# Low parts taken one half-block later at a stage's seam, and a fixed order for the last two tiles before the feed-forward part

## The chip, the cores and the metric

The kernel runs on one core of a Trainium2 chip. The time is device microseconds of that core for one launch, and a smaller time is better. Every time in this text is in microseconds unless it says ns.

The engines that matter here are TensorE (PE in the profile; PEld is its weight load), VectorE (DVE), ScalarE (ACT) and GpSimd (POOL). SyncE (SP) issues the transfers. Each engine takes its instructions in the order in which the program holds them for it, and an instruction waits on semaphores of the other engines and of transfers.

## The reference

One layer of a hybrid block works on 1024 tokens of width 1024 (16 meta tokens lead), all in float32. After a norm, one wide product gives the inputs of a pooling mixer and of a chunked, gated linear attention; both are merged under sigmoid gates and multiplied with `w_out`. A squared-ReLU feed-forward part of width 4096 and a last norm follow.

```python
h = h + hybrid_mixer(rmsnorm(h, norm_mix), ...)
#   y_a = pooling branch                      y_b = (attention output o) @ w_gla_out
#   m = sigmoid(ga) * y_a + sigmoid(gb) * y_b
#   returns m @ w_out
h = h + square(relu(rmsnorm(h, norm_ffn) @ w_ff1)) @ w_ff2
out = rmsnorm(h, norm_final)[:, N_META:]
```

## The kernel before

**Numbers.** A float32 value is kept as two parts that TensorE takes at full rate: a high part, which is a copy by ScalarE into a rounded type, and a low part, which is value minus high part, by VectorE (in some places by GpSimd). A product then is three matmuls for each 128 rows: high × high, low × high, high × low (`mm3`, L255 to L257 for the row numbers of its three matmuls). In the names, `th`/`tl` are high and low part of activations, `w1h`/`w1l` of weights in a ring of two slots (`Ring`, L83 and L87), `wo` holds both parts of half of `w_out`.

**The seam.** It lies between the attention and the product with `w_out`. `yb_block(n, h)` computes two blocks of 128 columns of `m` for the token half `h`; I call one of these a half-block (one value of `e`). It is 12 matmuls on `yg`, then on VectorE a multiplication with the gate (L1115), an addition of the pooling branch (L1116), the high part by ScalarE (L1119) and the low part, for `h = 1` by VectorE (L1121), for `h = 0` by GpSimd in four pieces (L1123). Gate and pooling branch are loaded from DRAM into buffers of three slots (`yb_load`, L1061 and L1062). In the second half, steps of `load_wo` stand between the blocks: each turns a quarter of the first half of `w_out` into its two parts (L1422, L1423). The third and fourth block of the second half need a new weight from the ring. After eight half-blocks, `out_tile` multiplies tile after tile of 128 tokens with `w_out`, first for columns 0 to 511 (`ch = 0`), then for the others.

**The opening of the feed-forward part.** In `out_tile` for `ch = 1` a tile is finished: its result is added to x (L1455), normed by `layer_norm` (L243 to L247), and two tiles later transposed by TensorE (`turn_tile`, L1472). The product with `w_ff1` is computed by a scheme with seven products of quarters instead of eight (P1 to P7, class `Quarters`), each 12 matmuls for half the rows of a block of 128 columns (4 times 128 rows, three matmuls each). Its operands are sums and differences of the four quarters of activations, so `turn_tile` for tiles 4 to 7 also computes differences: `t1` (L1482), which with its two parts (L1483, L1484) P5 reads, and after it four more arrays (L1477, L1486 to L1492) that only P6, P7 and P4 read. The weights' sums are made by `sums` and their two parts by `split` (L273, L274). For each weight pair the order is P1 P1 P2 P2 P5 P5 P6 P7 P4 P3 at the start. The last two tiles (6 and 7) are transposed between the first products, in `ff_layers`.

**What sets the order.** TensorE's order is that of the code. On the other engines a scheduler orders by its own estimates, except inside `in_order(...)` ... `any_order(...)`, where ScalarE, VectorE or SP also keep the order of the code. From the end of the attention to `wo1_open` ScalarE and VectorE are in such a stretch; `x_again`, `fetch_wo` and the loads around them are in one for SP. In the opening of the feed-forward part there is none.

Of the kernel before, what the change touches and what calls it, by code (L numbers as in the profile page):

```python
# [114 lines left out]
def kernel(  # L115
# [84 lines left out]
    def f32(ap):  # L200
        return ap.bitcast(F32)
# [4 lines left out]
    def bcast(v):  # L206
        return v[None, :].broadcast_to([P, D])
# [80 lines left out]
    class Quarters:  # L288
# [46 lines left out]
        def forms(self):  # L335

            for p, i, s in ahead(self.sums(), self.lead):
                yield p, i, split(s)
                if p == "P3" and i + 2 < self.n:
                    self.load(i + 2, 0)  # L340
                    self.load(i + 2, 1)
# [742 lines left out]

    kept = {}
    halves_of_half = [slice(k * HALF // 2, (k + 1) * HALF // 2) for k in range(2)]

    def yb_block(n, h):
        j = YB[h][n]

        def fn(*wbs):
# [6 lines left out]
            for e in range(2):  # L1098
                d, w = 2 * j + e, slice(e * P, (e + 1) * P)
                for m in range(2 + h):  # L1100
                    yb_load(2 * n + e + m, h)
                gl, ml = staged[2 * n + e, h]
                b = bank("mm")
                for k in range(4):
                    mm3(
                        b, 1, lambda i: (hi[:, k, w], lo[:, k, w]),
                        lambda i: (yg[:, 0, k], yg[:, 1, k]), first=k == 0, last=k == 3,
                    )
                    yield 3 * 512 / 2400
                if e and not wbs:  # L1110
                    W1.done, W1.kept = W1.done + 1, W1.kept - 1
                    W1.top_up()
                elif e:
                    yield "keep" if j in kept else "free"
                dve.tensor_tensor(gl, b, gl, ALU.mult)  # L1115
                dve.tensor_tensor(gl, gl, ml, ALU.add)  # L1116
                th = MH[h][:, d]
                tl = ML[h][:, d]
                act.activation(th, gl, ACT.Copy)  # L1119
                if h:  # L1120
                    dve.tensor_tensor(tl, gl, f32(th), ALU.subtract)  # L1121
                for c in halves_of_half[: 2 - 2 * h]:
                    pool.tensor_tensor(tl[:, c], gl[:, c], f32(th[:, c]), ALU.subtract)  # L1123
# [274 lines left out]

    def load_gB():
        nc.sync.dma_start(gB, bcast(norm_ffn))  # L1400

# [15 lines left out]
    def load_wo(ch, kk):  # L1417
        def fn():
# [3 lines left out]
            act.activation(wo[:, 0], r, ACT.Copy)  # L1422
            dve.tensor_tensor(wo[:, 1], r, f32(wo[:, 0]), ALU.subtract)  # L1423

# [36 lines left out]

    def turn_tile(t, tags=("ms",)):

# [16 lines left out]
        b12, t1 = (quad(acc[:, t, c]) for c in halves())  # L1480
        act.activation(b12, b[0], ACT.Copy)
        dve.tensor_tensor(t1, b[0], lo, ALU.subtract)  # L1482
        act.activation(MH[1][:, 0:4, cols], t1, ACT.Copy)  # L1483
        dve.tensor_tensor(ML[1][:, 0:4, cols], t1, f32(MH[1][:, 0:4, cols]), ALU.subtract)  # L1484
        split_from_psum(MH[1][:, 4:8, cols], ML[1][:, 4:8, cols], b[1])
        dve.tensor_tensor(lo, b[1], t1, ALU.subtract)  # L1486
        dve.tensor_tensor(b12, b[1], b12, ALU.subtract)
        dve.tensor_tensor(hi, hi, lo, ALU.subtract)
        for n, a in enumerate((lo, b12)):
            fh, fl = (S["wo"][0][:, k, 4 * n : 4 * n + 4, cols] for k in range(2))  # L1490
            act.activation(fh, a, ACT.Copy)
            dve.tensor_tensor(fl, a, f32(fh), ALU.subtract)  # L1492

# [27 lines left out]
    for t in ORDER[:6]:  # L1521
        step(one, out_tile(t, 1))
    step(one, lambda: ff_weights())
    for t in ORDER[6:]:
        step(one, out_tile(t, 1))
# [193 lines left out]
    def ff_layers():  # L1719
# [3 lines left out]
        run = ff_quarters.run()  # L1723
        for n in range(4):
            if n in (1, 3):
                turn_tile(ORDER[6 + n // 2])
            next(run)
# [53 lines left out]
```

## Time and profile before

| | us |
|---|---|
| median of 3 runs | 1224.9 |
| the runs | 1224.36 to 1225.51 |
| the profiled execution | 1225.56 |
| its span | 1222.7 |
| TensorE busy | 1202.0 |
| VectorE busy | 853.9 |
| ScalarE busy | 618.9 |
| GpSimd busy | 62.7 |

The profiled execution is one execution of the program, recorded by the hardware; its span runs from the first to the last instruction, and the execution's own time is 2.86 longer. Busy time of TensorE is the time in which a matmul is under way, and matmuls overlap, so that a matmul of 512 columns is recorded with 0.39 although the next one starts much sooner. Whether TensorE stands still is therefore read from the distance between starts. In a row of the timeline stand the start, the duration, the engine, the line, the operation, output and inputs with their shape, and in brackets how long the engine sat idle before it and who ended that.

In this trace the first half-block of the second token half reaches TensorE at about 484, the product with `w_out` starts at 506.67, the feed-forward part at 601.81.

### The profile page before, as it was taken

What the parts mean: (1) busy time and instruction counts of PE and PEld (TensorE: products, weight loads), DVE (VectorE), ACT (ScalarE), POOL (GpSimd) and SP (SyncE); (2) the same over time, 40 slices, a digit from 0 to 9 for tenths busy, and PEclk for the clock granted to TensorE, in tenths of its full rate; (3) what the DMA queues carried; (4) which work ended last, traced back from release to release, by engine and by line L of the source; (5) the groups of instructions that cost most, each with busy time, mean ns of one, the idle gap of its engine ahead of it and who ended that gap; (6) DMA issues with size and microseconds to landing.
All of it is one profiled execution on the core that took longest, in us unless ns stands there. A gap on an engine that the chain in (4) does not pass through costs nothing.

```text
span 1222.7 us, 18359 instructions
## 1 busy us (share of the span) xinstructions
PE 1202.0 (98%) x6818; PEld 1000.4 (82%) x6818; DVE 853.9 (70%) x1399; ACT 618.9 (51%) x1099; POOL 62.7 (5%) x100
## 2 busy tenths in 40 slices
PE   7999999999999999999999999999999999999997
PEld 7878888978888877788878888888888888888886
DVE  7986675754566677735887676676775887887686
ACT  7667567322546753323655455454554444444544
POOL 2000000001201225000000000000000000000000
PEclk9999999999999999999999999999999999999999
DMA  8043426156101246651244454444569973333532
GB/s 254 2 113 116 125 86 190 53 161 201 36 20 62 70 159 213 234 179 63 104 144 155 134 168 147 155 155 139 175 223 322 341 249 102 96 95 95 171 96 86
DMA packets 141672, 173.84 MB, mean 142 GB/s; under 512 B 9944, under 2 KB 81392, under 8 KB 141584
## 3 DMA queue, kind: packets, MB, share of 16 engines
q1 hardware_dynamic: 141552, 172.62, 43.6%
q8 instruction: 53, 0.87, 0.3%
q14 instruction: 35, 0.29, 0.1%
q0 software_dynamic: 32, 0.07, 0.0%
HBM read 119.17 MB, written 53.48 MB: 141 GB/s over the span
## 4 chain that ended last, share of the span: by engine, by line
PE 87%; DVE 7%; ACT 2%; issue 2%; DMA 1%; POOL 0%; SPq 0%; DVEq 0%; ACTq 0%; POOLq 0%
PE b_mm L255 10%; PE b_mm L256 10%; PE b_mm L257 10%; PE b_ms L256 9%; PE b_ms L255 9%; PE b_ms L257 9%; PE b_x L256 8%; PE b_x L255 8%; PE b_x L257 8%; PE b_sc L1207 1%; PE b_mx L255 1%; PE b_mx L256 1%; PE b_mx L257 1%; PE b_m L1309 1%; DVE ut L776 1%
## 5 line engine op out<-in xcount | busy, mean ns | idle before, releaser
L255 PE MATMUL b_mm<-th,w1h 128*128 128x512 f32 (+1 forms) x312 | 117.6, 377 | 1.6 <-DVE c L811 1.0
L256 PE MATMUL b_mm<-tl,w1h 128*128 128x512 f32 (+1 forms) x312 | 116.0, 372 | 0.6 <-DVE tl L1484 0.6
L257 PE MATMUL b_mm<-th,w1l 128*128 128x512 f32 (+1 forms) x312 | 115.9, 371 | 0.0
L255 PE MATMUL b_x<-th,w1h 128*128 128x512 f32 (+1 forms) x240 | 90.8, 378 | 0.0
L256 PE MATMUL b_x<-tl,w1h 128*128 128x512 f32 (+1 forms) x240 | 90.6, 378 | 0.0
L257 PE MATMUL b_x<-th,w1l 128*128 128x512 f32 (+1 forms) x240 | 90.3, 376 | 0.0
L273 ACT ACTIVATE w1h<-raw 128x512 fp32r<-128x512 f32 x96 | 59.5, 621 | 32.6 <-PE b_x L256 14.2
L274 DVE TENSOR_TENSOR w1l<-raw,w1h 128x512 fp32r<-128x512 f32 x96 | 65.6, 684 | 9.9 <-ACT w1h L273 9.9
L255 PEld LDWEIGHTS b_mm<-th,w1h 128*128 128x128 f32 x312 | 58.6, 188 | 13.2 <-issue 1.4
L273 ACT ACTIVATE w1h<-fs 128x512 fp32r<-128x512 f32 x72 | 45.4, 630 | 46.3 <-PE b_ms L256 31.8
L256 PEld LDWEIGHTS b_mm<-tl,w1h 128*128 128x128 f32 x312 | 58.6, 188 | 10.7 <-DVE tl L1484 0.9
L257 PEld LDWEIGHTS b_mm<-th,w1l 128*128 128x128 f32 x312 | 58.6, 188 | 10.3
L273 ACT ACTIVATE w1h<-bt 128x512 fp32r<-128x512 f32 x44 | 27.8, 632 | 67.1 <-issue 62.7
L274 DVE TENSOR_TENSOR w1l<-fs,w1h 128x512 fp32r<-128x512 f32 x72 | 49.3, 686 | 14.7 <-ACT w1h L273 14.6
L1638 DVE TENSOR_TENSOR bt<-w,w 128x512 f32<-128x512 f32 x80 | 54.6, 683 | 1.6 <-DMA w<-in_w_ff_dram 1.6
L257 PEld LDWEIGHTS b_x<-th,w1l 128*128 128x128 f32 x240 | 45.1, 188 | 8.5
L255 PEld LDWEIGHTS b_x<-th,w1h 128*128 128x128 f32 x240 | 45.1, 188 | 8.4
L256 PEld LDWEIGHTS b_x<-tl,w1h 128*128 128x128 f32 x240 | 45.1, 188 | 8.3
L273 ACT ACTIVATE fxh<-bt 128x512 fp32r<-128x512 f32 x36 | 22.8, 632 | 55.7 <-issue 50.1
L255 PE MATMUL b_ms<-wo,w1h 128*128 128x512 f32 x128 | 49.8, 389 | 0.0
L256 PE MATMUL b_ms<-wo,w1h 128*128 128x512 f32 x128 | 49.8, 389 | 0.0
L257 PE MATMUL b_ms<-wo,w1l 128*128 128x512 f32 x128 | 49.8, 389 | 0.0
(451 smaller groups left out, 3349.2 us busy)
## 6 DMA issues: line engine op xcount, KB each, us to landing
hf_dram<-h SPq DMA_DIRECT2D x112, 256.0 KB, 2.1
raw<-hf_dram SPq DMA_DIRECT2D x112, 256.0 KB, 2.6
w<-in_w_ff_dram SPq DMA_DIRECT2D x64, 256.0 KB, 4.7
raw<-in_w_in_dram SPq DMA_DIRECT2D x24, 512.0 KB, 4.8
raw<-in_w_ff_dram SPq DMA_DIRECT2D x16, 512.0 KB, 4.1
rawx<-in_w_ff_dram SPq DMA_DIRECT2D x16, 512.0 KB, 4.0
xs<-in_x_dram SPq DMA_DIRECT2D x8, 512.0 KB, 5.6
rawx<-in_w_in_dram SPq DMA_DIRECT2D x8, 512.0 KB, 4.4
```

Of the source, the lines that this page charges most:

```text
L255: pe.matmul(ps, ah, bh, start=first and i == 0, stop=False, skip_group_check=more)
L256: pe.matmul(ps, ah, bl, start=False, stop=False, skip_group_check=more)
L257: pe.matmul(ps, al, bh, start=False, stop=last and i == n - 1, skip_group_check=more)
L273: act.activation(hi, a, ACT.Copy)
L274: dve.tensor_tensor(lo, a, f32(hi), ALU.subtract)
L776: dve.tensor_tensor(to_, a_, b_, ALU.subtract)
L1207: pe.matmul(b[to, e, j], kk[r, s], qq[r, s], start=True, stop=True, tile_position=(e * CH, u * CH))
L1309: pe.matmul(o[part(u), e, j], scc[part(u), e, j], v[part(u), j, e], start=j == 0, stop=False, tile_position=(u * CH, u * CH), skip_group_c ...
L1638: dve.tensor_tensor(bt, w, S["w2"][q[3:]][:, i], ALU.add if q[2] == "+" else ALU.subtract)
```

## The change

The change has three parts.

First, in the seam, low parts are put into a list `pending` instead of being issued: that of a half-block of the second half (L1121 before), and those of `w_out` (L1423 before). `late()` issues what is in the list. It is called behind the multiplication of the next half-block; for the second half of `w_out` it is called at once, and the last one is issued before `gB` is loaded. The third load ahead for a half-block moves behind this point as well, since its buffer is what the late low part reads, and the ring's refill now stands between multiplication and addition.

VectorE, in the second half: the last row of the third weight block of the ring (`w1l`) and the half-blocks after it; `t` is a half-block's buffer, `o` the pooling branch. Before:

```order
L87 TENSOR_TENSOR w1l<-raw_115,w1h 128x1024
L1115 TENSOR_TENSOR t_4555<-b_mm,t_4555 128x512
L1116 TENSOR_TENSOR t_4555<-t_4555,o_4559 128x512
L1121 TENSOR_TENSOR tl_143<-t_4555,th_139 128x512
L1423 TENSOR_TENSOR wo_4843<-acc,wo_4843 128x1024
```

Now:

```order
L87 TENSOR_TENSOR w1l<-raw_115,w1h 128x1024
L1134 TENSOR_TENSOR t_4555<-t_4555,o_4559 128x512
L1124 TENSOR_TENSOR t_4555<-b_mm,t_4555 128x512
L1139 TENSOR_TENSOR tl_143<-t_4555,th_139 128x512
L1442 TENSOR_TENSOR wo_4843<-acc,wo_4843 128x1024
L1134 TENSOR_TENSOR t_4555<-t_4555,o_4559 128x512
```

Between a half-block's addition (now L1134) and its low part (now L1139) the multiplication of the next one (now L1124) stands, and that one's own addition comes only behind the weight's low part.

The first quarter of `w_out` is loaded early, and its low part stood on VectorE among the last half-blocks of the first token half, ahead of the sum of squares of the last attention part (L1331). Before:

```order
L1314 COPY small<-b_m_4670 128x2
L1115 TENSOR_TENSOR t_2709<-b_mm,t_2709 128x512
L1423 TENSOR_TENSOR wo_4843<-raw_4563,wo_4843 128x1024
L1116 TENSOR_TENSOR t_2709<-t_2709,o 128x512
L1331 TENSOR_REDUCE small<-mix 128x8
```

Now VectorE has it behind the first multiplication of the second half:

```order
L1133 TENSOR_TENSOR t_2709<-b_mx,t_2709 128x512
L1134 TENSOR_TENSOR t_2709<-t_2709,o 128x512
L1124 TENSOR_TENSOR t_4555<-b_mm,t_4555 128x512
L1442 TENSOR_TENSOR wo_4843<-raw_4563,wo_4843 128x1024
L1134 TENSOR_TENSOR t_4555<-t_4555,o_4559 128x512
```

It moved past the whole end of the attention, to where GpSimd still makes low parts of the first half.

Second, ScalarE and VectorE keep the order of the code from the last two tiles of `out_tile` to the third product of the feed-forward part. Third, in that stretch `turn_tile` leaves the differences that P6, P7 and P4 read to a function that is called later, `forms` can make a weight's sum ahead on demand (`pull`), and the last tile's transposes stand one product earlier on TensorE: behind the second P1 and no longer behind the first P2.

VectorE at the opening, from the last tile's norm (`u`, tile 7) on; `fs` is a sum of weights, the row of L1482 (now L1502) makes `t1`. Before (tile 6's `t1` stands just ahead of the piece):

```order
L247 SCALAR_TENSOR_TENSOR u_5026<-acc,small,gB 128x1024
L1484 TENSOR_TENSOR tl_143<-acc,th_139 128x4x128
L211 TENSOR_TENSOR tl_143<-b_ms,th_139 128x4x128
L1486 TENSOR_TENSOR acc<-b_ms,acc 128x512
L1487 TENSOR_TENSOR acc<-b_ms,acc 128x512
L1488 TENSOR_TENSOR acc<-acc 128x512
L1492 TENSOR_TENSOR wo_4843<-acc,wo_4843 128x4x128 x2
L274 TENSOR_TENSOR w1l<-fs,w1h 128x512
L1482 TENSOR_TENSOR acc<-b_ms,acc 128x512
L211 TENSOR_TENSOR tl_143<-b_ms,th_139 128x4x128
L1486 TENSOR_TENSOR acc<-b_ms,acc 128x512
L1484 TENSOR_TENSOR tl_143<-acc,th_139 128x4x128
```

Now:

```order
L247 SCALAR_TENSOR_TENSOR u_5026<-acc,small,gB 128x1024
L324 TENSOR_TENSOR fs<-raw_119 128x512
L1502 TENSOR_TENSOR acc<-b_ms,acc 128x512
L1504 TENSOR_TENSOR tl_143<-acc,th_139 128x4x128
L211 TENSOR_TENSOR tl_143<-b_ms,th_139 128x4x128
L274 TENSOR_TENSOR w1l<-fs,w1h 128x512
L1502 TENSOR_TENSOR acc<-b_ms,acc 128x512
L326 TENSOR_TENSOR fs<-fs,raw_115 128x512
L1504 TENSOR_TENSOR tl_143<-acc,th_139 128x4x128
L211 TENSOR_TENSOR tl_143<-b_ms,th_139 128x4x128
L324 TENSOR_TENSOR fs<-rawx_5695 128x512
L1509 TENSOR_TENSOR acc<-b_ms,acc 128x512
```

The low part of the last tile's `t1` (now L1504) stood behind tile 6's differences (L1486 to L1492) and is now ahead of them; both tiles' differences follow from the last row on, and the low parts for P4 (`t4l`, L1550 before), which stood ahead of P6's weight, now stand behind it.

The diff:

```diff
         def forms(self):
-            for p, i, s in ahead(self.sums(), self.lead):
+            due, made = [], self.sums()
+            self.pull = lambda: due.append(next(made))
+            while True:
+                while len(due) <= self.lead and (x := next(made, None)):
+                    due.append(x)
+                if not due:
+                    return
+                p, i, s = due.pop(0)
                 yield p, i, split(s)
...
-    kept = {}
+    kept, pending = {}, []
+
+    def late():
+        while pending:
+            pending.pop(0)()
...
-                for m in range(2 + h):
+                for m in range(2):
                     yb_load(2 * n + e + m, h)
...
+                if h:
+                    dve.tensor_tensor(gl, b, gl, ALU.mult)
+                    late()
+                    yb_load(2 * n + e + 2, h)
                 if e and not wbs:
                     W1.done, W1.kept = W1.done + 1, W1.kept - 1
                     W1.top_up()
                 elif e:
                     yield "keep" if j in kept else "free"
-                dve.tensor_tensor(gl, b, gl, ALU.mult)
+                if not h:
+                    dve.tensor_tensor(gl, b, gl, ALU.mult)
                 dve.tensor_tensor(gl, gl, ml, ALU.add)
...
                 if h:
-                    dve.tensor_tensor(tl, gl, f32(th), ALU.subtract)
+                    pending.append(lambda tl=tl, gl=gl, th=th: dve.tensor_tensor(tl, gl, f32(th), ALU.subtract))
...
     def load_gB():
+        late()
         nc.sync.dma_start(gB, bcast(norm_ffn))
...
             act.activation(wo[:, 0], r, ACT.Copy)
-            dve.tensor_tensor(wo[:, 1], r, f32(wo[:, 0]), ALU.subtract)
+            pending.append(lambda: dve.tensor_tensor(wo[:, 1], r, f32(wo[:, 0]), ALU.subtract))
+            if ch:
+                late()
...
-    def turn_tile(t, tags=("ms",)):
+    def turn_tile(t, tags=("ms",), later=None):
...
-        act.activation(b12, b[0], ACT.Copy)
         dve.tensor_tensor(t1, b[0], lo, ALU.subtract)
         act.activation(MH[1][:, 0:4, cols], t1, ACT.Copy)
         dve.tensor_tensor(ML[1][:, 0:4, cols], t1, f32(MH[1][:, 0:4, cols]), ALU.subtract)
         split_from_psum(MH[1][:, 4:8, cols], ML[1][:, 4:8, cols], b[1])
-        dve.tensor_tensor(lo, b[1], t1, ALU.subtract)
...
+        act.activation(b12, b[0], ACT.Copy)
+
+        def differences():
+            dve.tensor_tensor(lo, b[1], t1, ALU.subtract)
+            dve.tensor_tensor(b12, b[1], b12, ALU.subtract)
+            dve.tensor_tensor(hi, hi, lo, ALU.subtract)
+            for n, a in enumerate((lo, b12)):
+                fh, fl = (S["wo"][0][:, k, 4 * n : 4 * n + 4, cols] for k in range(2))
+                act.activation(fh, a, ACT.Copy)
+                dve.tensor_tensor(fl, a, f32(fh), ALU.subtract)
+
+        if later is None:
+            differences()
+        else:
+            later.append(differences)
...
     step(one, lambda: ff_weights())
+    step(one, lambda: in_order("order", mybir.EngineType.Activation, mybir.EngineType.DVE))
     for t in ORDER[6:]:
         step(one, out_tile(t, 1))
...
-        for n in range(4):
-            if n in (1, 3):
-                turn_tile(ORDER[6 + n // 2])
+        later = []
+        for n in range(5):
+            if n == 1:
+                ff_quarters.pull()
+                turn_tile(ORDER[6], later=later)
+            elif n == 2:
+                turn_tile(ORDER[7], later=later)
+                ff_quarters.pull()
+                later[0]()
+            elif n == 3:
+                later[1]()
+                any_order("order")
             next(run)
```

More of the change, by code (lines that the diff above doesn't have):

```diff
@@ L1485, in turn_tile @@
         split_from_psum(MH[1][:, 4:8, cols], ML[1][:, 4:8, cols], b[1])
-        dve.tensor_tensor(lo, b[1], t1, ALU.subtract)
[L1487 to L1492, printed above, removed]
+        act.activation(b12, b[0], ACT.Copy)
[11 more added lines that the diff above has]
+            later.append(differences)
     for n, j in enumerate(YB[1]):
```

## The prediction

> **What bounds the kernel now.** I read the head of the page and its chain first, then the list of waits of TensorE, then the timelines of TensorE, VectorE, ScalarE and GpSimd around the two places that the change touches. Times inside the trace are microseconds from the start of the span.
>
> ```profile
> span 1222.7 us, 18359 instructions
> PE 87%; DVE 7%; ACT 2%; issue 2%; DMA 1%; POOL 0%; SPq 0%; DVEq 0%; ACTq 0%; POOLq 0%
> ```
>
> TensorE carries the chain. Only time in which it stands still can be won, and the list of its waits shows single waits of under a microsecond, two of them at the lines of the change:
>
> ```profile
> PE b_mm L256 <- DVE wo L1423: 0.8, 1, 0.8
> PE b_mm L256 <- DVE tl L1484: 0.6, 1, 0.6
> ```
>
> A wait costs more than its own length, since the first matmul after it is spaced wider. So I measure from start to start. The seam, on TensorE:
>
> ```profile
> 484.34 0.39 PE L255 MATMUL b_mm<-yg,w1h 128*128 128x512 f32 x1
> 485.04 0.50 PE L256 MATMUL b_mm<-yg,w1h 128*128 128x512 f32 x1 [0.31 <-DVE yg L1341]
> 485.38 0.39 PE L257 MATMUL b_mm<-yg,w1l 128*128 128x512 f32 x1
> ...
> 499.46 0.39 PE L256 MATMUL b_x<-yg,w1h 128*128 128x512 f32 x1
> 499.68 0.39 PE L257 MATMUL b_x<-yg,w1l 128*128 128x512 f32 x1
> 500.27 0.50 PE L255 MATMUL b_x<-yg,w1h 128*128 128x512 f32 x1 [0.20 <-ACT w1h L83]
> ...
> 501.53 0.50 PE L257 MATMUL b_x<-yg,w1l 128*128 128x512 f32 x1 [0.53 <-DVE w1l L87]
> 501.86 0.40 PE L255 MATMUL b_x<-yg,w1h 128*128 128x512 f32 x1
> ...
> 510.52 0.39 PE L257 MATMUL b_mm<-wo,tl 128*128 128x512 f32 x1
> 511.38 0.50 PE L255 MATMUL b_mm<-wo,th 128*128 128x512 f32 x1 [0.47 <-ACT wo L1422]
> 512.64 0.50 PE L256 MATMUL b_mm<-wo,th 128*128 128x512 f32 x1 [0.76 <-DVE wo L1423]
> 512.98 0.40 PE L257 MATMUL b_mm<-wo,tl 128*128 128x512 f32 x1
> ```
>
> Undisturbed matmuls follow each other at 0.227 (499.46 to 499.68, and the like all over). Lost are therefore: at yg 485.38 − 484.34 − 2 × 0.227 = 0.59; at the third weight block 501.86 − 499.68 − 4 × 0.227 = 1.27; at the last quarter of w_out 512.98 − 510.52 − 3 × 0.227 = 1.78. That is **3.64 in the seam**. The feed-forward opening:
>
> ```profile
> 597.31 0.39 PE L257 MATMUL b_mm<-wo,tl 128*128 128x512 f32 x1
> 598.16 1.06 PE L1472 MATMUL b_ms<-ident,u 128*128 128x128 f32 x8 [0.46 <-DVE small L220]
> ...
> 614.28 0.39 PE L257 MATMUL b_x<-th,w1l 128*128 128x512 f32 x1
> 615.28 0.49 PE L255 MATMUL b_mm<-th,w1h 128*128 128x512 f32 x1 [0.61 <-ACT th L1483]
> 616.41 0.50 PE L256 MATMUL b_mm<-tl,w1h 128*128 128x512 f32 x1 [0.64 <-DVE tl L1484]
> 616.75 0.40 PE L257 MATMUL b_mm<-th,w1l 128*128 128x512 f32 x1
> ```
>
> Before the transposes 598.16 − 597.31 − 0.227 = 0.62 is lost; at the fifth product (P5) 616.75 − 614.28 − 3 × 0.227 = 1.79. All five together are 6.05, 0.5% of the span: no more than that can be won here. The profiled execution took 1225.56, 0.66 above the median of 1224.9; I take the difference from the trace and put it on the median.
>
> **The change, part by part.**
>
> *Low parts taken one half-block later.* One half-block of before on VectorE and ScalarE, and a half-block without a weight behind it:
>
> ```profile
> 501.39 0.68 DVE L1115 TENSOR_TENSOR t<-b_mm,t 128x512 f32<-128x512 f32 x1
> 502.11 0.69 DVE L1116 TENSOR_TENSOR t<-t,o 128x512 f32<-128x512 f32 x1
> 502.83 0.63 ACT L1119 ACTIVATE th<-t 128x512 fp32r<-128x512 f32 x1 [2.62 <-DVE t L1116]
> 503.37 1.04 ACT L1422 ACTIVATE wo<-acc 128x1024 fp32r<-128x1024 f32 x1
> 504.45 1.23 DVE L1423 TENSOR_TENSOR wo<-acc,wo 128x1024 fp32r<-128x1024 f32 x1 [0.26 <-ACT wo L1422]
> 505.59 0.68 DVE L1115 TENSOR_TENSOR t<-b_mm,t 128x512 f32<-128x512 f32 x1
> ...
> 507.70 0.69 DVE L1121 TENSOR_TENSOR tl<-t,th 128x512 fp32r<-128x512 f32 x1 [0.70 <-ACT th L1119]
> 508.31 0.68 DVE L1115 TENSOR_TENSOR t<-b_x,t 128x512 f32<-128x512 f32 x1
> ```
>
> The period of VectorE is 505.59 − 501.39 = 4.20 with a weight and 508.31 − 505.59 = 2.72 without; TensorE's is 12 × 0.227 = 2.72. So every weight puts VectorE 1.48 further behind, which is why the last quarter of w_out is late. In the period VectorE stands idle 0.70 for the high part of the block and 0.26 for that of the weight. In the new order it multiplies the next half-block in that gap. Count from an addition's start: the next multiplication follows at 0.61 (507.70 to 508.31 is the spacing of two that don't depend on each other). The high part starts at 0.72 and is there at 1.39; the low part runs 1.39 to 2.00; the weight's low part, which is 504.45 − 502.83 = 1.62 behind the start of the block's high part, starts at 2.34 and ends at 2.34 + 1.14 = 3.48, where the next addition starts. The period becomes 3.48 and 2.00: **0.72 less per half-block**.
>
> *The first quarter of w_out leaves its old place.*
>
> ```profile
> 470.57 1.21 DVE L1423 TENSOR_TENSOR wo<-raw,wo 128x1024 fp32r<-128x1024 f32 x1
> 471.70 1.23 DVE L1116 TENSOR_TENSOR t<-t,o 128x512 f32<-128x512 f32 x1
> ...
> 487.05 3.73 POOL L1123 TENSOR_TENSOR tl<-t,th 128x256 fp32r<-128x256 f32 x4 [3.15 <-ACT th L1119]
> ...
> 487.55 0.68 DVE L1115 TENSOR_TENSOR t<-b_mm,t 128x512 f32<-128x512 f32 x1
> 488.27 1.21 DVE L1116 TENSOR_TENSOR t<-t,o 128x512 f32<-128x512 f32 x1
> ```
>
> The addition at 471.70 goes up by 1.13, and with it the high part behind it on ScalarE, the square of the last attention part behind that, and the chain that ends in yg. Yg's wait was 0.59, so it vanishes, and the first multiplication of the second half comes at about 486.4 instead of 487.55. There w_out's low part is put in: 1.14, and since GpSimd is then in its four low parts, 0.52 more, as the addition at 488.27 pays (1.21 against 0.69). The addition pays 0.52 too: it starts at 486.4 + 0.61 + 1.66 = 488.7, the next at 488.7 + 3.48 + 0.52 = 492.7, then 496.2 and 499.7, which is the end of the third weight block's low part. TensorE wants it with the third matmul, 499.68 + 3 × 0.227 = 500.36, now less 0.59: 499.8. So it comes just in time. Bounds: nothing is lost if GpSimd is out of the way, 1 if all three instructions on VectorE wait longer; I take 0.3, nearest to the row of 488.27. The last quarter of w_out ends at 499.7 + 3.48 + 2.00 + 3.48 = 508.7; it is wanted at 510.52 + 0.45 − 0.59 − 1.27 + 0.3 = 509.4, in time by 0.7. Seam: −3.64 + 0.3 = **−3.3**.
>
> A rule against this change: the Trainium skill, "SBUF — State Buffer", section "Who interferes with whom", says that a VectorE instruction with two inputs in SBUF and a GpSimd instruction that reads SBUF exclude each other for their whole length. The trace shows a longer addition (1.21 against 0.69), but not a full block of a GpSimd quarter, 3.73 / 4 = 0.93. By the row the seam gives 3.3; by the rule it gives what the first rival below says.
>
> *Loads.* The two loads of a half-block (256 KB each) are now issued behind the late low part, as their buffer is read by it, and on SP's fixed order a w_out fetch stands behind some of them. A load issued at an addition + 2.0 is wanted two multiplications later, 3.6 behind it at the tightest. One landing in the chain, and the loads of x:
>
> ```profile
> 491.36 3.57 DMA t<-gb_dram
> ```
> ```profile
> acc<-in_x_dram SPq DMA_DIRECT2D x8, 512.0 KB, 8.9
> ```
>
> 3.57 just fits; I take nothing for it.
>
> *Opening, fixed order.* The transposes of the last tile move up by one product on TensorE, 12 × 0.227 = 2.72. VectorE and ScalarE take both tiles' first difference and parts for P5 before all that only P6 and P7 need. That removes P5's 1.79: VectorE needs about four instructions fewer (4 × 0.6 = 2.4) ahead of the last tile's low part. But VectorE's work up to P6 hardly gets less. In before it has
>
> ```profile
> 619.29 1.28 DVE L1550 TENSOR_TENSOR t4l<-acc,t4h 128x512 fp32r<-128x512 f32 x2
> 620.49 0.68 DVE L274 TENSOR_TENSOR w1l<-fs,w1h 128x512 fp32r<-128x512 f32 x1
> ```
>
> so P6's weight is there at 621.2. The order now puts the two t4l behind it, −1.2; but waits in fixed order come in, one of 1.39 − 0.61 = 0.78 where one instruction stands between a difference and its low part, one of 0.18 where two do: ready at 621.0. TensorE, no longer held at P5, wants it with P6's third matmul, 614.28 + 27 × 0.227 = 620.4. Wait 0.6 and 0.1 for the wider start; between 0 and the 1.79 of before I take 0.9, as ScalarE's order adds waits that this count leaves out. The transposes' 0.62 can grow by one VectorE instruction put ahead of the row statistics (0 to 0.61): +0.3. Opening: −1.79 + 0.9 + 0.3 = **−0.6**.
>
> *What costs nothing.* The x loads follow the last yb load and move up with it; x is added into results that free a bank only four tiles later. The reordered `sums` beyond the opening leave TensorE's order as it was, and after 630 the trace has no wait on these weights.
>
> Sum: −3.3 − 0.6 = −3.9. Span 1222.7 − 3.9 = 1218.8; median 1224.9 − 3.9 = **1221.0**.
>
> **Rivals.** *GpSimd holds VectorE.* If w_out's low part, the addition and the next low part each wait out a whole GpSimd instruction (0.93), 3 × 0.93 − 2 × 0.52 = 1.75 is added; the third weight block comes 1.8 late, 1.9 with the wider start, and the seam gives 3.64 − 1.9 = 1.7. With the opening −2.3: 1222.6, within 0.2%. For it: every such instruction inside GpSimd's stretch is long in the trace. Against: long by 0.5, not 0.93. The rule quoted above is this rival.
>
> *Loads come late, slower than before.* With a landing of 8.9, as the x loads have, the load behind the sixth half-block would be 8.9 − 3.6 = 5.3 late, the last w_out part stands behind that multiplication, and TensorE waits 5.3 − 0.7 = 4.6 there, and once more about 1 at the third block: −3.9 + 5.6 = +1.7, 1226.6. It decides from a landing of about 3.6 + 0.7 + 3.9 = 8.2. Against: the x loads are long because eight stand in a row, and they stay behind.
>
> *The opening gives nothing.* P6 waits as long as P5 did (1.79) and the transposes 0.61 more: −3.3 + 0.6 = −2.7, 1222.2, still faster.
>
> *The change does not do what it says* can be left out: the order printed for VectorE has the low parts where the diff puts them.
>
> **How the numbers follow.** Forecast 0.76 (1220.2 to 1221.8 by the bounds 0 to 1 and 0 to 1.79), opening gives nothing 0.09, GpSimd 0.10, loads 0.05 of which 0.02 is only part of that price and within 0.2%. A measurement of this kernel can tell about 0.2%, 2.45. Faster is the forecast and the opening's rival, 0.85; within 0.2% the GpSimd rival and the partial late loads, 0.12; slower 0.03. The range takes in both rivals that stay below 1224.9, and below it the case that the opening loses nothing at P6 (−4.8): 1219.9 to 1222.9.
>
> **What would show it.** Right: no wait on wo L1442 and none on yg; at most one of 0.3 on the third block's low part; addition to addition 3.5 with a weight and 2.0 without; no wait on th at P5, one of 0.5 to 0.9 on a weight's low part at P6. Wrong: VectorE idle on a DMA between 490 and 508; w_out's first low part longer than 1.8; a wait at P6 of over 1.5.

## The result and the profile after

The changed kernel takes 1222.87 us (median of 22 runs, 1222.16 to 1225.95), the kernel before in the same series 1225.12 (22 runs). The ratio is 0.9983, 95% interval 0.9977 to 0.9989: 2.2 us or 0.17% faster, where 3.9 us were forecast. The profiled span fell from 1222.7 to 1220.7.

The list of TensorE's waits of the changed kernel (total, times, longest) no longer has the waits on `wo` and on `yg` and `th`. The longest that it has at the two places of the change stand at P6 and ahead of the transposes:

```profile
PE b_ms L257 <- DVE w1l L274: 0.6, 1, 0.6
PE b_ms L1493 <- DVE small L220: 0.6, 1, 0.6
```

I measure losses as the prediction does, from start to start against 0.227 a matmul. The timeline of the changed kernel, TensorE, at the third weight block, P5, P6 and P3:

```profile
499.26 0.39 PE L257 MATMUL b_x<-yg,w1l 128*128 128x512 f32 x1
...
501.34 0.50 PE L257 MATMUL b_x<-yg,w1l 128*128 128x512 f32 x1 [0.52 <-DVE w1l L87]
501.68 0.39 PE L255 MATMUL b_x<-yg,w1h 128*128 128x512 f32 x1
...
615.41 0.39 PE L255 MATMUL b_mm<-th,w1h 128*128 128x512 f32 x1
...
616.21 0.39 PE L255 MATMUL b_mm<-th,w1h 128*128 128x512 f32 x1
...
618.50 0.39 PE L256 MATMUL b_ms<-wo,w1h 128*128 128x512 f32 x1
619.47 0.50 PE L257 MATMUL b_ms<-wo,w1l 128*128 128x512 f32 x1 [0.59 <-DVE w1l L274]
619.81 0.39 PE L255 MATMUL b_ms<-wo,w1h 128*128 128x512 f32 x1
...
627.09 0.39 PE L257 MATMUL b_ms<-t4h,w1l 128*128 128x512 f32 x1
627.93 0.47 PE L255 MATMUL b_mm<-th,w1h 128*128 128x512 f32 x1 [0.45 <-ACT w1h L273]
628.23 0.39 PE L256 MATMUL b_mm<-tl,w1h 128*128 128x512 f32 x1
```

| lost by TensorE, us | before | after | forecast for after |
|---|---|---|---|
| yg | 0.59 | 0 | 0 |
| third weight block: 501.68 − 499.26 − 4 × 0.227 | 1.27 | 1.51 | 0.3 |
| last quarter of `w_out` | 1.78 | 0 | 0 |
| transposes: 596.34 − 595.38 − 0.227 | 0.62 | 0.73 | 0.9 |
| P5: 616.21 − 615.41 − 3 × 0.227 | 1.79 | 0.12 | 0 |
| P6: 619.81 − 618.50 − 2 × 0.227 | 0 | 0.86 | 0.9 |
| P3: 628.23 − 627.09 − 2 × 0.227 | 0 | 0.69 | 0 |

Two rows are off by much: the third weight block, which got no better at all, and P3, which was not on the list. What leads to the first, on the other engines of the changed kernel:

```profile
486.33 4.76 POOL L1141 TENSOR_TENSOR tl<-t,th 128x256 fp32r<-128x256 f32 x4 [3.15 <-ACT th L1137]
...
487.43 1.22 DVE L1442 TENSOR_TENSOR wo<-raw,wo 128x1024 fp32r<-128x1024 f32 x1
488.56 1.22 DVE L1134 TENSOR_TENSOR t<-t,o 128x512 f32<-128x512 f32 x1
...
491.11 0.38 SPq L1433 DMA_DIRECT2D acc<-in_w_out_dram  x1
...
495.50 1.06 ACT L1441 ACTIVATE wo<-acc 128x1024 fp32r<-128x1024 f32 x1 [1.46 <-DMA t<-gb_dram]
496.59 1.23 DVE L1442 TENSOR_TENSOR wo<-acc,wo 128x1024 fp32r<-128x1024 f32 x1 [1.83 <-ACT wo L1441]
```

GpSimd's four low parts start 0.72 earlier than before (487.05) but take 4.76 in place of 3.73, and end at 491.09. SP issues the load of `w_out`'s second quarter 0.02 later; it goes into `acc`, whose memory holds the buffers that GpSimd still reads. In each of the eight traces in which GpSimd has all these pieces and this load keeps its place, the load is issued 0.02 to 0.03 behind GpSimd's end, in the kernel before too (490.78 and 490.81). ScalarE stands 1.46 for it (the bracket names another load, but L1441 reads `acc`), VectorE 1.83, and the third block's low part follows one half-block behind, at 500.06. "VectorE idle on a DMA between 490 and 508" was the sign that the forecast named for being wrong.

### The profile page after: what moved, and what is told of

Read it like the earlier page. It is cut to its first block, busy times and chain, and to the rows that moved or that the text cites. A ratio compares the mean times of both kernels' runs of the same rounds, so it can differ in the third digit from the quotient of the medians.

```text
span 1220.7 us, 18354 instructions
## 1 busy us (share of the span) xinstructions
PE 1202.3 (98%) x6818; PEld 1001.6 (82%) x6818; DVE 853.7 (70%) x1399; ACT 618.3 (51%) x1099; POOL 63.2 (5%) x100
## 4 chain that ended last, share of the span: by engine, by line
PE 88%; DVE 7%; ACT 3%; issue 1%; DMA 1%; POOL 0%; SPq 0%; DVEq 0%; ACTq 0%; POOLq 0%
PE b_mm L255 11%; PE b_mm L256 10%; PE b_mm L257 10%; PE b_ms L257 9%; PE b_ms L255 9%; PE b_ms L256 9%; PE b_x L257 8%; PE b_x L256 8%; PE b_x L255 8%; PE b_sc L1225 1%; PE b_mx L255 1%; PE b_mx L256 1%; PE b_mx L257 1%; PE b_m L1327 1%; DVE ut L783 1%
```

## The experiments

Theory 1: GpSimd's end sets the load, the load sets the third weight block, and GpSimd ends late because `w_out`'s first low part was put among its four pieces. Rival A: GpSimd is slow for another reason. Rival B: the block is late by its own chain of instructions. Rival C: the transfer takes its time whenever it starts. For P3, theory 2: it waits for an addition on VectorE that stands behind a sum waiting for a load; the rival is what the profile's bracket says, a weight on ScalarE.

### One part alone

The two parts of the diff taken apart: the seam's hunks alone, and the hunks of `forms`, `turn_tile` and `ff_layers` alone.

> Only the seam's part of the change, the opening of the feed-forward as before. By the losses of the matrix engine in the two traces the seam went from 3.64 us plus 0.15 (transposes) to 1.50, so this kernel should take nearly all of the gain: 2.0 to 2.3 us under the kernel before, about 1222.9. By the recorded forecast's split (seam -3.3, opening -0.6) with an unknown loss in the opening it would be 3.3 under, 1221.8.

> Only the opening's part, the seam as before. By the losses in the two traces (wait at P5 1.79 gone to about 0.15; new 0.85 at P6; new 0.6 to 0.7 at the first matmul of P3 at 627.93; transposes 0.1 longer) it gains 0.0 to 0.2 us: 1224.9 to 1225.1, no change that can be measured. By the recorded forecast it gains 0.6 and nothing is late after P6: 1224.5.

Seam alone: 1222.80, ratio 0.9983 (0.9974 to 0.9992). Opening alone: 1225.01 beside 1225.03, ratio 1.0001 (0.9992 to 1.0010). The whole gain is the seam's; the opening gives nothing that can be told. In this trace of the opening alone P3 waits too, and the bracket names another instruction, the addition on VectorE (L1591 is the line of L1605 in the changed kernel):

```profile
630.29 0.47 PE L255 MATMUL b_mm<-th,w1h 128*128 128x512 f32 x1 [0.32 <-DVE h L1591]
```

### The low part later in GpSimd's stretch

```diff
                     dve.tensor_tensor(gl, b, gl, ALU.mult)
-                    late()
+                    if (n, e) != (0, 0):
+                        late()
```

> After, but the low part of w_out's first quarter is held one multiplication longer, so that VectorE does it once GpSimd's four low parts are over; the first half-block's own low part goes with it. Theory 1 (the load of w_out's second quarter is held by GpSimd, whose four pieces grew from 3.73 to 4.76 us because this 1.22 us VectorE instruction was put among them): the four pieces take 3.3 to 3.8, the load is issued at 489.9 to 490.3 in place of 491.1, the matrix engine's loss at the third weight block falls from 1.50 to 0.3 to 0.6, the time by about 1.0 us to 1221.9. Rival A (GpSimd is slowed by the additions and multiplications around it, not by this instruction): the pieces stay above 4.4, the loss at 1.2 or more. Rival B (the block is late by its own chain of addition, high part, weight's high part, weight's low part, 3.48 us a half-block, not by the load): the loss stays at 1.5 even if the load is earlier.

1222.22, ratio 0.9974 (0.9964 to 0.9985). The timeline:

```profile
486.47 3.73 POOL L1142 TENSOR_TENSOR tl<-t,th 128x256 fp32r<-128x256 f32 x4 [3.15 <-ACT th L1138]
...
489.55 1.73 DVE L1443 TENSOR_TENSOR wo<-raw,wo 128x1024 fp32r<-128x1024 f32 x1
...
490.22 0.38 SPq L1434 DMA_DIRECT2D acc<-in_w_out_dram  x1
...
495.05 1.06 ACT L1442 ACTIVATE wo<-acc 128x1024 fp32r<-128x1024 f32 x1 [0.77 <-DMA t<-gb_dram]
...
499.39 0.39 PE L257 MATMUL b_x<-yg,w1l 128*128 128x512 f32 x1
...
501.24 0.39 PE L255 MATMUL b_x<-yg,w1h 128*128 128x512 f32 x1
```

GpSimd is back at 3.73, what it took before the change, so rival A falls: the 1.03 go with the instruction that was moved. It did not leave GpSimd's stretch altogether: it starts at 489.55, 0.65 ahead of GpSimd's end, and here it is VectorE that pays, 1.73 in place of 1.22. The load is issued 0.89 earlier, but ScalarE starts only 0.45 earlier, and the loss is 501.24 − 499.39 − 4 × 0.227 = 0.94: a gain of 0.57 and not the 0.9 to 1.2 that I expected. Part of what the earlier issue gives is lost in the transfer: 495.05 − 490.22 = 4.83 from issue to use, against 495.50 − 491.11 = 4.39. The intervals of this ratio and of the changed kernel's overlap, so the gain rests on the trace more than on the time.

### Two pieces fewer on GpSimd

```diff
+                if not h and (n, e) == (3, 1):
+                    dve.tensor_tensor(tl, gl, f32(th), ALU.subtract)
+                    continue
                 if h:
```

> After, but the last of the two half-blocks that GpSimd takes at the end of the first pass has its low part made on VectorE in one instruction, right after its high part. GpSimd then has two pieces in place of four and ends near 488.5; the load no longer waits for its last two. Theory 1: the load is issued at 488.3 to 488.8, ScalarE's high part of w_out's second quarter starts right behind the half-block's high part (about 494, no wait for a transfer), the loss at the third weight block is 0 to 0.2, and the time is 1.2 to 1.5 us under the changed kernel, about 1221.5, unless the 1.4 us that VectorE now stands or works more at 487 to 488.3 comes back at the second weight block. Rival B (own chain): the loss at the third block stays near 1.5 or grows by what VectorE does more. Rival C (the transfer takes longer because of its neighbours in the queues, whenever it starts): issue is 2.6 us earlier, but the landing less than 1 us earlier, and the loss stays above 0.7.

1221.80, ratio 0.9974 (0.9963 to 0.9984).

```profile
486.06 2.91 POOL L1144 TENSOR_TENSOR tl<-t,th 128x256 fp32r<-128x256 f32 x2 [3.15 <-ACT th L1137]
...
488.30 1.22 DVE L1139 TENSOR_TENSOR tl<-t,th 128x512 fp32r<-128x512 f32 x1
...
489.65 0.38 SPq L1436 DMA_DIRECT2D acc<-in_w_out_dram  x1
...
494.55 1.06 ACT L1444 ACTIVATE wo<-acc 128x1024 fp32r<-128x1024 f32 x1 [0.28 <-DMA t<-gb_dram]
...
498.99 0.39 PE L257 MATMUL b_x<-yg,w1l 128*128 128x512 f32 x1
...
500.73 0.40 PE L255 MATMUL b_x<-yg,w1h 128*128 128x512 f32 x1
```

The time came near the expectation, the mechanism only in part. GpSimd ends at 488.97, but now VectorE's low part, which stands behind `w_out`'s, holds the load until 489.65. From issue to use it takes 4.90, and the loss is 0.83, where 0 to 0.2 was expected. So the third block gives 0.68 of the 1.07 by which the time fell. Another 0.40 came at P3, which loses 0.29 in this trace (626.95 − 626.21 − 2 × 0.227) though the edit does not touch it: the time came out near by luck.

Up to here rival C has the long transfers for it (4.39, 4.83, 4.90), and rival B can still claim the remaining 0.8. That the transfer is longer the earlier it is issued does not follow: in four kernels whose seam is the same it takes 4.34 (the seam alone), 4.39 (the changed kernel), 4.59 and 4.80 (the two kernels for the opening further down), and the loss at the third block is 1.47, 1.51, 1.71 and 2.09. One trace against another is therefore good to some 0.6 at this place, and the differences of 0.57 and 0.68 are of that size.

### The load freed

The last row tile of `acc` becomes a buffer of its own, over memory that GpSimd does not read, and takes this load. On VectorE, ScalarE and GpSimd the order stays as in the changed kernel; of the loads, this one comes earlier, and the fourth quarter's goes to the place that this one had.

```diff
-        S["acc"] = left.push("acc", [P, 8, D], F32)
+        S["acc"] = Slots([left.push(f"acc{i}", [P, n, D], F32) for i, n in enumerate((7, 1))])
...
-        fetch_wo(0, 1, S["acc"][:, 5])
+        fetch_wo(0, 1, S["acc"][:, 7])
...
-            step(one, lambda kk=n + 2: fetch_wo(0, kk, S["acc"][:, 4 + kk]))
+            step(one, lambda kk=n + 2: fetch_wo(0, kk, S["acc"][:, 8 - kk]))
```

> After, with one transfer moved and nothing else: the load of w_out's second quarter goes into the last of the eight row tiles of acc, kept as a buffer of its own over memory that the low parts of GpSimd do not read, so it needs not wait for GpSimd. VectorE's, ScalarE's and GpSimd's orders stay. Theory 1 (GpSimd holds the load): the load is issued at about 482 to 483 in place of 491.1, GpSimd still takes about 4.8 us, ScalarE's high part of the quarter starts right behind the half-block's high part (about 494) and waits for no transfer; the matrix engine's loss at the third weight block falls from 1.50 to what the half-block chain itself leaves, 0.3 to 0.7 by the two runs that shortened the wait; time 0.8 to 1.2 us under the changed kernel, 1221.7 to 1222.1. Rival C (the landing is long whenever it starts): would need a landing of over 11 us to matter. Rival B (own chain alone): loss stays at 1.5.

1220.94, ratio 0.9966 (0.9954 to 0.9979).

```profile
476.47 0.39 SPq L1433 DMA_DIRECT2D acc<-in_w_out_dram  x1
...
486.50 4.76 POOL L1141 TENSOR_TENSOR tl<-t,th 128x256 fp32r<-128x256 f32 x4 [3.16 <-ACT th L1137]
...
494.12 1.05 ACT L1441 ACTIVATE wo<-acc 128x1024 fp32r<-128x1024 f32 x1
...
498.68 1.23 DVE L87 TENSOR_TENSOR w1l<-raw,w1h 128x1024 fp32r<-128x1024 f32 x1 [0.26 <-ACT w1h L83]
...
499.25 0.39 PE L257 MATMUL b_x<-yg,w1l 128*128 128x512 f32 x1
...
500.30 0.39 PE L255 MATMUL b_x<-yg,w1h 128*128 128x512 f32 x1
```

The load is issued at 476.47, earlier still than expected (482 to 483) and about 10 us ahead of GpSimd's pieces. GpSimd is as slow as in the changed kernel, ScalarE waits for nothing, and the loss is 500.30 − 499.25 − 4 × 0.227 = 0.14. Rival B falls with it: the chain of the half-blocks is in time by itself, and better than I had expected after the two runs before (0.3 to 0.7); the time too is below what was expected. The span is 1.3 shorter than that of the changed kernel, as the loss says (1.51 − 0.14); the medians differ by 1.9, and the 0.6 between these I leave unexplained.

### One GpSimd piece more

```diff
-                for c in halves_of_half[: 2 - 2 * h]:
+                for c in halves_of_half[: 2 - 2 * h] + ([halves_of_half[1]] if not h and (n, e) == (3, 1) else []):
```

> The changed kernel, and GpSimd does the last of its four low parts twice (the same values again). Theory 1: the load of w_out's second quarter is issued 0.8 to 1.2 us later, at 491.9 to 492.3, and the matrix engine's loss at the third weight block grows by as much, from 1.50 to 2.3 to 2.7; time 1223.6 to 1224.0. If instead the load's landing is set by the transfers issued beside it (rival C), the loss grows by less than 0.4.

1223.84, ratio 0.9989 (0.9980 to 0.9997).

```profile
486.18 5.90 POOL L1141 TENSOR_TENSOR tl<-t,th 128x256 fp32r<-128x256 f32 x5 [3.15 <-ACT th L1137]
...
492.11 0.38 SPq L1433 DMA_DIRECT2D acc<-in_w_out_dram  x1
...
499.11 0.39 PE L257 MATMUL b_x<-yg,w1l 128*128 128x512 f32 x1
...
502.53 0.39 PE L255 MATMUL b_x<-yg,w1h 128*128 128x512 f32 x1
```

The load comes 1.00 later, the loss is 502.53 − 499.11 − 4 × 0.227 = 2.51, also 1.00 more, the span 1.0 longer and the time 0.97. A microsecond on GpSimd at this place was a microsecond of the kernel. That it comes out so exactly is in part chance, as the transfer alone differs by more between traces, and the intervals of the two ratios overlap. Rival C, in the strong form that I had given it, falls.

### The quarter's high part one half-block earlier

On top of the free load, ScalarE makes the high part of this quarter ahead of the second half-block's high part.

```diff
                     W1.top_up()
+                    if n == 0:
+                        load_wo(0, 1)()
...
-        step(one, load_wo(0, n))
+        if n != 1:
+            step(one, load_wo(0, n))
```

> As the kernel with the free load, and ScalarE makes the high part of w_out's second quarter one half-block earlier, ahead of the second half-block's high part, in the 2 us in which it stood idle before 493.4. If what the free load leaves is the half-block chain (addition, high part, w_out's high part, w_out's low part, next addition), VectorE's idle time ahead of w_out's low part goes, the third weight's low part comes 0.5 us earlier or more, and the matrix engine's loss there falls to 0 to 0.2; time 1.3 to 1.6 us under the changed kernel, 1221.3 to 1221.6. If the chain is held elsewhere (the third weight's own high part or load), the loss stays where the free load leaves it.

1220.95, ratio 0.9967 (0.9955 to 0.9980): the same as the free load alone, and below the 1221.3 to 1221.6 that I had expected. TensorE's loss at the third block is gone, but there were only 0.14 left to take.

### P3: the order or the transfer

Two kernels on top of the free load move the seven stores of the first half-sums (`hf_dram<-h`) from SP's queue to GpSimd's, and to ScalarE's (`nc.scalar` in the same place).

```diff
-            nc.sync.dma_start(hf_of[w][i], S["h"][:, i % 2, w])
+            (nc.gpsimd if i == 0 else nc.sync).dma_start(hf_of[w][i], S["h"][:, i % 2, w])
```

> The kernel with the free load (1220.94), and the seven stores of the first half-sums to memory that stood on SP's queue go out on GpSimd's queue instead. In the kernel before this one the two raw blocks for the sum at 626 were issued with two such stores between them. Without them the second is issued about 0.9 us earlier. Theory 2 (P3's first matmul waits for the addition that empties its bank, which stands on VectorE behind a sum that waits for that raw block): the sum waits 0 to 0.1 in place of about 0.45, the loss at P3 falls from 0.69 to 0.2 to 0.3, the time by 0.4 to 1220.5. Rival (P3 waits for a later product's weight on ScalarE): the loss stays at 0.69.

> The same stores on ScalarE's queue. By the built order this also makes VectorE do the addition that empties P3's bank ahead of the sum (before it now), so neither the sum's wait nor its 0.60 stands ahead of it. Theory 2: the loss at P3 goes from 0.69 to 0 to 0.1, the time by 0.5 to 0.7, to 1220.3. Rival (weight on ScalarE): the loss stays or grows, since ScalarE now issues stores too.

On GpSimd's queue 1220.44, ratio 0.9962 (0.9948 to 0.9975); on ScalarE's 1220.73, 0.9963 (0.9951 to 0.9976). First the changed kernel, VectorE ahead of P3's first matmul at 627.93:

```profile
626.49 0.69 DVE L324 TENSOR_TENSOR fs<-raw 128x512 f32<-128x512 f32 x1 [0.45 <-DMA raw<-in_w_ff_dram]
627.10 0.68 DVE L1605 TENSOR_TENSOR h<-b_mm,u3p 128x512 f32<-128x512 f32 x1
```

Then the stores on GpSimd's queue, VectorE, ScalarE and TensorE:

```profile
624.03 0.69 DVE L324 TENSOR_TENSOR fs<-raw 128x512 f32<-128x512 f32 x1
624.64 0.68 DVE L1605 TENSOR_TENSOR h<-b_mm,u3p 128x512 f32<-128x512 f32 x1
...
625.03 0.39 PE L257 MATMUL b_ms<-t4h,w1l 128*128 128x512 f32 x1
...
625.23 0.63 ACT L273 ACTIVATE w1h<-s 128x512 fp32r<-128x512 f32 x1 [2.86 <-PE b_ms L256]
...
625.47 0.47 PE L255 MATMUL b_mm<-th,w1h 128*128 128x512 f32 x1
625.77 0.40 PE L256 MATMUL b_mm<-tl,w1h 128*128 128x512 f32 x1
```

The sum (L324) no longer waits for its raw block, and P3's loss is 625.77 − 625.03 − 2 × 0.227 = 0.29. On ScalarE's queue, where the addition (L1605) is done ahead of the sum, it is 626.21 − 625.55 − 2 × 0.227 = 0.21, where 0 to 0.1 was expected. The weight on ScalarE that the bracket of the changed kernel names (`w1h<-s`) is done only at 625.23 + 0.63 = 625.86 here, and P3 has started at 625.47, so P3 does not wait for it. And whichever engine the bracket names, P3's first matmul starts 0.15 behind the end of this addition: in the changed kernel (627.78 and 627.93), in these two (625.32 and 625.47, 625.75 and 625.90), and in the traces of the opening alone, the free load, the earlier high part and the kernel with all that helped. Theory 2 holds: P3 adds to a bank that P5's result must first be read from, and the reader stood behind a wait for a transfer. In time this is 0.5 and 0.2 against 1220.94, which these series can't tell from nothing: the intervals of the ratios overlap.

### Two ways to mend the opening that did not work

The fixed order kept longer, so that the addition would come first:

```diff
                 later[1]()
-                any_order("order")
             next(run)
         ff_room()
-        for _ in run:
-            pass
+        for n, _ in enumerate(run):
+            if n == 5:
+                any_order("order")
```

> After, with the fixed order of ScalarE and VectorE kept seven products longer in the opening of the feed-forward. In the changed kernel the first matmul of P3 (627.93, 0.61 late) needs P5's bank to have been read by the addition at 627.10; that addition stands on VectorE behind the sum for a later product at 626.49, which waited 0.45 for its two raw blocks and takes 0.6. In written order the addition comes first. Theory 2 (the order set free too early put a wait for a transfer ahead of the addition): the 0.61 and the 0.1 behind it go, 1222.1 to 1222.3. Rival (the weight of a later product on ScalarE at 627.29 is what P3 waits for, as the profile names it): the loss stays.

1232.76, ratio 1.0064 (1.0052 to 1.0077): 9.9 slower than the changed kernel. The steps that follow are written as pairs of which each waits for the other engine, and in written order VectorE and ScalarE take turns at waiting (VectorE stood 2.99 for one weight's high part). P3 then came 4.0 late, and the matmuls behind it were slow themselves. Timeline, and below it a window (busy time of each engine with its instructions, then the granted clock, 0.50, and the transfers):

```profile
635.64 0.76 PE L255 MATMUL b_mm<-th,w1h 128*128 128x512 f32 x1 [4.00 <-DVE h L1605]
636.20 0.63 PE L256 MATMUL b_mm<-tl,w1h 128*128 128x512 f32 x1
```
```profile
636.00:640.00 4.00, 4.00 (x10) 3.08 (x10) 1.90 (x3) 2.50 (x5) 0.00 (x0) 0.50 0.35 131
```

The second one makes P6's first operand and P6's weight before the rest of the last tile's steps:

```diff
             elif n == 3:
-                later[1]()
-                any_order("order")
+                later[2]()
             next(run)
+            if n == 3:
+                later[3]()
+                any_order("order")
```

> After, with the last tile's steps in halves: P6's first operand, P6's weight's low part, then the rest. In the changed kernel the low part of P6's weight stands on VectorE behind 3 differences and 2 low parts and is 0.74 plus 0.11 late. Here two instructions of 0.60 and one low part of 0.60 fewer stand ahead of it: it comes 1.2 to 1.8 us earlier and the 0.85 goes, 1222.0 to 1222.2, if nothing else is late at P6; if the matrix engine there waits for the operands that it reads from wo, 0.3 to 0.6 stay. The loss at the first matmul of P3 stays or grows, because VectorE has as much to do by then.

1225.12, ratio 0.9999 (0.9990 to 1.0008): all of the gain is lost again. I had moved the end of the fixed order behind `next(run)` as well, and in that call the sum for P6's weight is made. In the changed kernel the scheduler, free by then, had drawn that sum forward to 609.50; here it stands where it is written, and P6's weight waits for it:

```profile
620.16 0.69 DVE L326 TENSOR_TENSOR fs<-fs,raw 128x512 f32<-128x512 f32 x1
620.88 0.63 ACT L273 ACTIVATE w1h<-fs 128x512 fp32r<-128x512 f32 x1 [1.77 <-DVE fs L326]
621.57 0.51 PE L255 MATMUL b_ms<-wo,w1h 128*128 128x512 f32 x1 [1.08 <-ACT w1h L273]
```

TensorE loses 2.05 there. It loses 1.50 at P5 as well, where the second block's weight waits on ScalarE behind the high part of a difference, and 2.09 at the third weight block, which the edit does not touch. So neither run says whether P6's 0.86 can be had; that stays open.

### All that helped, together

The free load, the earlier high part and the stores on ScalarE's queue, by the diffs above.

> The free load, w_out's second high part one half-block earlier, and the stores of the first half-sums on ScalarE's queue, together. If the three losses are apart from each other, the seam loses nothing (0.1 at most), P3 nothing, P6 0.85 still: 1220.3 to 1220.5, 2.4 us under the changed kernel and 4.6 under the one before.

1220.49, ratio 0.9960 (0.9948 to 0.9973): 2.4 under the changed kernel, 4.7 under the kernel before, and no better than the free load with the stores on GpSimd's queue.

## Why the prediction was wrong

**The step that failed is "Loads".** "3.57 just fits; I take nothing for it" looked at the loads of a half-block and let the quarter of `w_out` pass. Its load ends in a wait for GpSimd, and that had to be followed: GpSimd's four pieces 4.76, issue 491.11, use 495.50, TensorE's loss at the third weight block 1.51, where 0.3 was forecast. With the load freed the loss is 0.14, within the forecast's 0 to 1 and below its 0.3. The miss in the seam is 1.51 − 0.3 = 1.2 us. Of the 1.37 that the free load wins, 0.57 went when GpSimd's pieces took 3.73 again; the other 0.80 are there because the load stands behind GpSimd at all, and by the scatter between traces this split is rough.

The wait stood in the trace of before, SP's queue and ScalarE:

```profile
490.81 0.38 SPq L1414 DMA_DIRECT2D acc<-in_w_out_dram  x1
...
494.96 1.06 ACT L1422 ACTIVATE wo<-acc 128x1024 fp32r<-128x1024 f32 x1 [0.50 <-DMA t<-gb_dram]
```

ScalarE stood 0.50 for this load there (the bracket again names another one). The forecast took 0.72 per half-block off the chain of low parts, but nothing in the change made the load earlier by as much: 490.81 before, 491.11 after.

**"Just in time" was right, in part by luck.** With the load freed the third weight's low part ends at 498.68 + 1.23 = 499.9, and 499.7 was forecast. But the first multiplication of the second half starts at 487.00 in that trace (486.83 in the changed kernel), where 486.4 was forecast: it moved up by 0.5 to 0.7 and not by 1.13. And `w_out`'s low part, charged with 0.52, paid nothing. The two errors cancel.

**Contention was in part put on the wrong engine.** The forecast charged VectorE 0.52 for `w_out`'s low part and 0.52 for the addition, and GpSimd nothing. In the changed kernel that low part takes 1.22, as at 496.59 where GpSimd is idle (1.23). The addition paid 0.53 (1.22 against 0.69), and so did the low part behind it (1.15 against 0.69), as it had before the change. GpSimd paid beside `w_out`'s low part, with one piece of 1.76 in the changed kernel; the longest is 1.19 when the low part comes later. The pieces of both kernels, by line (shortest, median, longest, ns), first the changed one:

```profile
L1141 POOL TENSOR_TENSOR tl<-t,th x4: 741/1186/1764, 486.3 to 490.3; 128x256 fp32r<-128x256 f32 x4
```
```profile
L1142 POOL TENSOR_TENSOR tl<-t,th x4: 729/956/1187, 486.5 to 489.5; 128x256 fp32r<-128x256 f32 x4
```

The rival "GpSimd holds VectorE" was therefore near the result, 1222.6 against 1222.87, but by luck: beside `w_out`'s low part VectorE held GpSimd, and the third block was late by a load. By the busy windows of GpSimd the long piece starts at about 487.46, 0.03 behind VectorE's low part (487.43). In the kernel that takes this low part later, the low part starts at 489.55, about 0.09 behind GpSimd's last piece, and there VectorE takes 1.73 and the piece 0.73. Each time the one that started later paid. The Trainium skill, "SBUF — State Buffer", section "Who interferes with whom", also says that it is the order of issue that decides which of the two is held; these two cases agree, and the longest piece, 1.76 − 0.74 = 1.02 over the shortest, was held for almost the whole of VectorE's 1.22.

**The opening: four terms, one forgotten.** P5's 1.79 went as forecast (0.12 left), P6's new wait is 0.86 against 0.9, and the transposes' bracket grew by 0.11 against 0.3. "After 630 the trace has no wait on these weights" was the wrong step: once TensorE ran earlier there, P3 met an addition that stood behind VectorE's wait for a transfer, 0.69. Against 2.41 of losses before (0.62 + 1.79) stand 0.12 + 0.86 + 0.69 + 0.73 = 2.40, which is the zero that the opening alone measured. The rival "the opening gives nothing" had this sum but not its mechanism: P6 lost 0.86 and not 1.79, and P3, which it does not name, lost the rest.

**Right** were the end of the wait for yg, the last quarter of `w_out`, and the periods. VectorE's additions of the changed kernel behind the late load are 3.48, 3.47 and 3.47 apart with a weight and 2.00 without, where 3.48 and 2.00 were forecast (497.73, 501.21, 504.68, 506.68, 510.15). In the sum: 3.9 less 1.2 for the load and 0.6 for the opening is 2.1, and 2.2 was measured. 1222.87 still lies at the edge of the range, 1219.9 to 1222.9, which took in the rivals. The narrower 1220.2 to 1221.8 is not what its bounds give: 0 to 1 at the third block and 0 to 1.79 at P6 make 1219.8 to 1222.6.

## What to carry to other kernels

In these traces a load went out only behind the last reader of the memory that it goes into; when work is moved, look up which loads wait for the engine next to which it now runs, not only how that work itself is slowed. An engine that is 5% busy can carry the critical path: one microsecond more on GpSimd here cost about one microsecond of the kernel. When a wait is removed, the next wait in line on the same engine has to be priced too. And a fixed order kept too long can cost more than it gives: seven products more cost 9.9 here.

## What I had not expected of the hardware

Where an instruction of GpSimd and one of VectorE met, the loss was not shared: a VectorE instruction of 1.22 passed undisturbed and the GpSimd piece next to it grew from 0.74 to 1.76, and in another kernel the same instruction, started behind a GpSimd piece, grew to 1.73 while the piece took 0.73.

A transfer of 512 KB, the same one each time, took from issue to use between 4.10 (the opening alone) and 4.90 (two pieces fewer) in the nine traces in which ScalarE waited for it, and 4.34 to 4.80 in the four with the same seam. The cause was not tried.

After TensorE had waited 4.0 us, its matmuls were 0.43 apart (636.20 to the next at 636.63) in place of 0.227, at a granted clock of 0.50 in the window from 636 to 640. The Trainium skill, "TensorE: Matmul & The Clock Gate", section "Part 1: The HAM clock gate", states half the clock after about 3.4 us of idleness; the trace agrees, with 0.50 behind a wait of 4.00, while the waits of 1.58 and 2.13 at 620 and 628 in the same kernel left the clock at 1.00.
